# A hybrid decoder trunk: the output projection's low parts pinned behind the conv taps, and the conv finish traced inside the attention

## The chip, the cores and the metric

The kernel runs on one core of a Trainium2 chip. The core has a matrix engine (TensorE, PE in the profile, whose weight loads are listed as PEld), a vector engine (VectorE, DVE), a scalar engine (ScalarE, ACT), a general engine (GpSimd, POOL) and a queue that issues DMAs (SyncE, SP). Every engine works through its own instructions in the order fixed when the program is built; semaphores make one wait for another. The metric is the time of one execution in device microseconds, as the median of several runs.

## The reference

Two layers act on a sequence of 512 rows of 1024 features. Each layer is a half-weighted SwiGLU, a token mixer and a second half-weighted SwiGLU, all residual and behind an RMS norm. The mixer is:

```python
a, g, q, k, v = jnp.split(h @ w_in[l], splits, axis=-1)
conv_out = conv_module(a, g, conv_w[l], conv_b[l], conv_norm[l])
...
diff_out = diff_attention(q, k, v, rel_bias, lam, lam_init, subln_norm[l])
x = x + jnp.concatenate([conv_out, diff_out], axis=-1) @ w_out[l]
```

`conv_module` gates `a` with the sigmoid of `g`, convolves each of 512 channels with its own 31 taps, causally, norms over the channels and applies `silu`. `diff_attention` has four heads; each has two softmax maps over the same 512 positions, causal and with a shared bias, and its value weights are the first map minus `lam` times the second. The result is normed per head. The output projection takes 512 conv features and 512 attention features.

## The kernel before

All matrix products are done in three passes. A weight chunk of 128 x 1024 is loaded (`wraw`), ScalarE writes its rounded high part (`whi`, L97) and VectorE or GpSimd the rest (`wlo`, L98); activations have the same two parts (`acth`, `actl`). `mm3` adds high x high (L160), high x low part of the activations (L163) and low part of the weights x high (L164). Rings hold five raw chunks and four high and four low parts. `chunk` (L100) issues the load on SP's queue and makes both parts.

The mixer first forms the conv inputs and the queries, keys and values. Then `conv_taps` (L652) runs over the four channel tiles: tile 0 wholly on GpSimd (31 taps), tile 3 with 10 taps there, the rest on VectorE. A tap on GpSimd is a product on ScalarE (`prod`, L662, a ring of two) and an add on GpSimd (L663). `conv_square` adds up the squares in `csum` (L650).

The attention is a software pipeline of 16 steps (four blocks of 128 queries from the last to the first, four heads each). `attend(n)` does, for step n, the two score products on PE (`ps_sc`, L709, in the PSUM banks `sc` and `po`), the bias add with a running minimum on VectorE (L713), the exponentials on ScalarE (L717), and the joining of both maps on VectorE (`r2` L720, `c2` L722, then L723); for step n-2 the transposes (`ps_at`, L730, copied by L732), for step n-3 the products with the values (`ps_o`, L739), and after the last head of a block its norm and its transposes into the activations (L766, L768, L769).

`conv_finish` (L684) sums the rows of `csum` by transposes (`rows_rstd`: L216, L220, L221 and a power on GpSimd, L209), spreads the result over the partitions (`spread`: a diagonal on VectorE L236, a product on PE L240, a copy on ScalarE L244), and for each tile scales on GpSimd (L689), takes a tanh on ScalarE (L691), and makes the gated value and its two parts (L692 on VectorE, L693 on ScalarE, L694 on VectorE).

The output projection (L810 on) adds the conv half first, for all rows, in eight tiles (`ps_out`, in the same banks `sc` and `po`, added to `x` by L820), and then the attention half in two row halves. Its weight chunks' low parts are made on GpSimd. After it the next SwiGLU's activations are prepared tile by tile (L257, L258).

The order of the instructions on each engine isn't the order of the text. A planner simulates the program and gives each engine the ready instruction that was traced first, so an instruction that is traced late can be placed early if its inputs are ready and its engine is free in the plan. `keep_in_program_order` pins an instruction behind the one traced just before it on its engine.

Of the kernel before, what the change touches and what calls it, by code (L numbers as in the profile page):

```python
# [15 lines left out]
ALU = mybir.AluOpType  # L16
# [11 lines left out]
CC = 512  # L28
# [39 lines left out]
def trunk(ctx: ExitStack, tc: tile.TileContext, xt, par, lamv, relb, onehot,  # L68
          gu1, dn1, wag, wqkv, wout, gu2, dn2, out):
    nc = tc.nc  # L70
    V, S, G, T = nc.vector, nc.scalar, nc.gpsimd, nc.tensor
# [9 lines left out]
    def f32(ap):  # L81
        return ap.bitcast(F32)
# [3 lines left out]
    def bank(tag, name):  # L86
        return psum.tile([P, 512], F32, tag=tag, name=name, bufs=BANKS[tag])
# [5 lines left out]
        dt = F32 if "raw" in tag else F32R  # L93
        return wp.tile([P, n], dt, tag=tag, name=tag, bufs=RING[tag])

    def parts_of(raw, hi, lo, eng=None):
        S.activation(hi, raw, AF.Copy)  # L97
        (eng or V).tensor_tensor(out=lo, in0=raw, in1=f32(hi), op=ALU.subtract)  # L98

    def chunk(src, eng=None):  # L100
        raw, hi, lo = ring("wraw"), ring("whi"), ring("wlo")
        nc.sync.dma_start(raw, src)
        parts_of(raw, hi, lo, eng)
        return hi, lo

    def gather(src, blocks, eng=None):
# [79 lines left out]
    for k0, k1 in ((0, 1), (1, 4), (4, KT)):  # L186
        h = slice(k0 * P, k1 * P)
# [24 lines left out]
    def rows_rstd(s, dim, use="", pin=False):  # L212

        ps = bank("y", "ps_rows")
        for j in range(NT):
            mm = T.transpose(ps[:, j * P : (j + 1) * P], s[:, j * P : (j + 1) * P], ident)  # L216
            if pin:
                tc.keep_in_program_order(mm)
        v = small.tile([P, NT], F32, tag=f"rowv{use}", name="rowv")
        V.tensor_reduce(v, ps.rearrange("p (j c) -> p j c", j=NT), axis=AX.X, op=ALU.add)  # L220
        V.tensor_scalar(v, v, 1.0 / dim, EPS, op0=ALU.mult, op1=ALU.add)  # L221
        return rsqrt(v, NT, use), v

    def spread(rc, tag, pin=False, split=False):

        parts, dt, left = [rc], F32, ones
        if split:
            hi = small.tile([P, NT], F32R, tag="rc_hi", name="rc_hi")
            V.tensor_scalar(hi, rc, 1.0, None, op0=ALU.mult)
            lo = small.tile([P, NT], F32, tag="rc_lo", name="rc_lo")  # L230
            V.tensor_tensor(lo, rc, f32(hi), op=ALU.subtract)
            parts, dt, left = [f32(hi), lo], F32R, ones_r
        ps = bank("y", "ps_spread")
        for n, part in enumerate(parts):
            dg = tmp.tile([P, NT, P], dt, tag=("diag", "sq")[n], name="diag", bufs=1 + n)
            V.tensor_tensor(  # L236
                dg, ident.unsqueeze(1).broadcast_to([P, NT, P]),
                part.unsqueeze(2).broadcast_to([P, NT, P]), op=ALU.mult,
            )
            mm = T.matmul(ps, left, dg.rearrange("p j c -> p (j c)"), start=n == 0, stop=n == len(parts) - 1)  # L240
            if pin:
                tc.keep_in_program_order(mm)
        r = act.tile([P, SEQ], F32, tag=tag, name=tag)
        S.activation(r, ps, AF.Copy)  # L244
        return r
# [254 lines left out]
    nlam, gq, gsub, ghalf = [], [], [], []  # L500
# [35 lines left out]
    def mixer(l, pr, after):  # L536
        with tc.tile_pool(name="mix", bufs=1) as mp, tc.tile_pool(name="mt", bufs=2) as mt:
# [104 lines left out]
            csum = mp.tile([P, SEQ], F32, tag="csum", name="csum")  # L642
# [9 lines left out]
            def conv_taps(c, n):  # L652

                wc = _AT["conv_w"] + c * TAPS
                yp = None
                if n:
                    yp = mp.tile([P, SEQ], F32, tag="yp%d" % (n < TAPS), name="yp")
                    G.tensor_scalar(yp, us[c][:, 0:SEQ], pars[l][:, wc : wc + 1], col(l, "conv_b", c),
                                    op0=ALU.mult, op1=ALU.add)
                    for t in range(1, n):  # L660
                        p = mt.tile([P, SEQ], F32, tag="prod", name="prod")
                        S.activation(p, us[c][:, t : t + SEQ], AF.Copy, scale=pars[l][:, wc + t : wc + t + 1])  # L662
                        G.tensor_tensor(yp, yp, p, op=ALU.add)  # L663
                if n == TAPS:
                    ys[c] = yp
                    conv_square(c, yp)
                    return
                y = bank("y", "ps_y")
                if not n:
                    V.tensor_scalar(y, us[c][:, 0:SEQ], pars[l][:, wc : wc + 1], col(l, "conv_b", c),  # L670
                                    op0=ALU.mult, op1=ALU.add)
                else:
                    V.tensor_scalar(y, us[c][:, n : n + SEQ], pars[l][:, wc + n : wc + n + 1], None, op0=ALU.mult)
                for t in range(n + 1 if n else 1, TAPS):
                    V.scalar_tensor_tensor(y, us[c][:, t : t + SEQ], pars[l][:, wc + t : wc + t + 1], y,
                                           op0=ALU.mult, op1=ALU.add)
                ys[c] = us[c][:, PAD:]
                if n:
                    V.tensor_tensor(ys[c], y, yp, op=ALU.add)
                else:  # L680
                    S.activation(ys[c], y, AF.Copy)
                conv_square(c, ys[c])

            def conv_finish():  # L684
                rcv = spread(rows_rstd(csum, CC, "c")[0], "rb")
                for c in range(CT):
                    z = ys[c]
                    hg = ghalf[l][:, c : c + 1]
                    G.tensor_tensor(z, z, rcv, op=ALU.mult)  # L689
                    th = mt.tile([P, SEQ], F32, tag="gl", name="th", bufs=1)  # L690
                    S.activation(th, z, AF.Tanh, scale=hg)  # L691
                    V.scalar_tensor_tensor(z, th, 1.0, z, op0=ALU.add, op1=ALU.mult)  # L692
                    S.activation(ch[:, c, :], z, AF.Copy, scale=hg)  # L693
                    V.scalar_tensor_tensor(cl[:, c, :], z, hg, f32(ch[:, c, :]), op0=ALU.mult, op1=ALU.subtract)  # L694
# [5 lines left out]
            def softmaxes(i, h):  # L700
                W = (i + 1) * P
                tq = slice(i * P, W)
                if h == 0:
                    sums[i] = small.tile([P, 2, HEADS], F32, tag="sums", name="sums")
                scs = [bank(tag, "ps_sc")[:, :W] for tag in ("sc", "po")]
                e0 = mt.tile([P, SEQ], F32, tag="e0", name="e", bufs=4)[:, :W]
                sm = sums[i]
                for m in range(2):
                    T.matmul(scs[m], qz[:, m, h, tq], kt[:, h, :W], start=True, stop=True)  # L709

                for m, (sc, e) in enumerate(zip(scs, (e0, scs[1]))):
                    mn = small.tile([P, 1], F32, tag=f"mn{m}", name="mn")
                    V.tensor_tensor_reduce(  # L713
                        out=e, in0=sc, in1=row["bias"][:, h, SEQ - W :], scale=1.0, scalar=3e38,
                        op0=ALU.add, op1=ALU.min, accum_out=mn,
                    )
                    S.activation(e, e, AF.Exp, bias=mn, scale=-1.0, accum_out=sm[:, m, h : h + 1])  # L717

                r2 = small.tile([P, 1], F32, tag="r2", name="r2")
                V.reciprocal(r2, sm[:, 1, h : h + 1])  # L720
                c2 = small.tile([P, 1], F32, tag="c2", name="c2")
                V.tensor_scalar(c2, r2, nlam[l], sm[:, 0, h : h + 1], op0=ALU.mult, op1=ALU.mult)  # L722
                V.scalar_tensor_tensor(e0, scs[1], c2, e0, op0=ALU.mult, op1=ALU.add)  # L723
                maps[i, h] = e0

# [75 lines left out]
                project_values(NT - 2 - 2 * n)  # L801
            for c in range(CT):
                conv_taps(c, POOL_TAPS[c])
            for n in range(2, len(steps) + 5):
                attend(n)
            conv_finish()

            for half, t in ((0, slice(0, SEQ)), (1, slice(SEQ // 2, SEQ)), (1, slice(0, SEQ // 2))):  # L810
                if t.stop == SEQ:
                    w = [None] * 4
                for m in range(KT):
                    if w[m // 2] is None:
                        w[m // 2] = chunk(wout[l, half, m // 2], G)
                    ps = bank(("sc", "po")[m % 2], "ps_out")[:, : t.stop - t.start]
                    for kk in range(4):
                        k = half * 4 + kk
                        mm3(ps, wpart(w[m // 2], (m % 2) * 4 + kk), (ch[:, k, t], cl[:, k, t]), kk == 0, kk == 3)
                    V.tensor_tensor(x[:, m, t], ps, x[:, m, t], op=ALU.add)  # L820

                    if half == 1 and t.start == 0 and m < KT // 2:
                        after(m)
# [103 lines left out]
```

## Time and profile before

| | |
|---|---|
| median of 3 runs | 1797.14 us (1795.66 to 1797.37) |
| the profiled execution | 1795.63 us |
| its span | 1793.9 us, 28355 instructions |
| PE busy | 1783.0 us, 99% |
| DVE, ACT, POOL busy | 67%, 50%, 37% |
| granted TensorE clock | 1.00 |

Times in the rows are microseconds from the start of the span, unless they are given as ns. A timeline row reads: start, length, engine, line, operation, out<-in, form and count, and in brackets the engine's idle time before it and what ended that. A group's row gives the count, then the busy time in us and the mean of one in ns, then the idle time before them. A row of one line's instructions gives the count and the least, median and greatest duration in ns. A row of stretches gives for each engine the busy time in it and the number of instructions.

### The profile page before, as it was taken

The numbers are of one execution on the slowest core, as the hardware profiler recorded it, in microseconds if no ns is written. First come the engines' busy times: TensorE is split into PE (matmuls) and PEld (weight loads), VectorE is DVE, ScalarE is ACT, GpSimd is POOL, SyncE is SP. The second block draws the span as 40 slices with busy tenths as digits, with TensorE's granted clock in tenths as the row PEclk, the third lists the DMA queues.
The fourth block names the chain that finished last, engine by engine and source line by source line (L and its number), as shares of the span: only waits on it lengthen the run. The fifth ranks groups of instructions, "written<-read, shape, count | busy, mean of one in ns | idle before, by whom it ended". The sixth has DMA issues, their size and how long they took to land.

```text
span 1793.9 us, 28355 instructions
## 1 busy us (share of the span) xinstructions
PE 1783.0 (99%) x10845; PEld 1590.0 (89%) x10845; DVE 1207.6 (67%) x1862; ACT 897.1 (50%) x1482; POOL 666.8 (37%) x460
## 2 busy tenths in 40 slices
PE   9999999999999999999999999999999999999999
PEld 7899899888788899899888998998887888998997
DVE  6977476568867867477576764765788587663762
ACT  5555265445844456266433643644558354552651
POOL 4243242269843133133102312412797332422420
PEclk9999999999999999999999999999999999999999
DMA  7466476423212367366334664663231133664651
GB/s 243 109 171 188 108 185 173 123 89 94 71 48 83 94 165 189 105 171 191 104 94 98 171 167 123 178 175 118 71 116 50 48 106 93 166 177 112 180 150 59
DMA packets 111721, 231.24 MB, mean 129 GB/s; under 512 B 12151, under 2 KB 33414, under 8 KB 111584
## 3 DMA queue, kind: packets, MB, share of 16 engines
q1 hardware_dynamic: 91488, 191.93, 33.4%
q0 software_dynamic: 19808, 37.33, 12.8%
q8 instruction: 85, 1.39, 0.3%
q14 instruction: 52, 0.43, 0.1%
q10 hardware_dynamic: 288, 0.16, 0.0%
HBM read 227.26 MB, written 3.42 MB: 129 GB/s over the span
## 4 chain that ended last, share of the span: by engine, by line
PE 96%; DVE 2%; ACT 1%; issue 1%; DMA 0%; ACTq 0%; DVEq 0%
PE ps_pair L379 38%; PE ps_d L164 9%; PE ps_d L160 9%; PE ps_d L163 9%; PE ps_pair L163 5%; PE ps_pair L164 5%; PE ps_pair L160 5%; PE ps_pair L592 2%; PE ps_pair L593 2%; PE ps_pair L591 2%; PE ps_out L160 1%; PE ps_out L163 1%; PE ps_sc L709 1%; PE ps_out L164 1%; DVE actl L258 1%; PE ps_v L623 1%
## 5 line engine op out<-in xcount | busy, mean ns | idle before, releaser
L97 ACT ACTIVATE whi<-wraw 128x512 fp32r<-128x512 f32 (+2 forms) x600 | 467.2, 802 | 607.5 <-PE ps_pair L379 223.2
L98 DVE TENSOR_TENSOR wlo<-wraw,whi 128x512 fp32r<-128x512 f32 (+2 forms) x556 | 521.3, 960 | 212.5 <-ACT whi L97 207.3
L379 PE MATMUL ps_pair<-acth,wlo 128*128 128x256 f32 x1088 | 307.9, 283 | 0.0
L379 PE MATMUL ps_pair<-actl,whi 128*128 128x256 f32 x1088 | 307.9, 283 | 0.0
L379 PE MATMUL ps_pair<-acth,whi 128*128 128x256 f32 x1088 | 307.9, 283 | 0.0
L163 PE MATMUL ps_d<-hl,whi 128*128 128x512 f32 x704 | 273.9, 389 | 0.0
L164 PE MATMUL ps_d<-hh,wlo 128*128 128x512 f32 x704 | 273.0, 389 | 0.0
L160 PE MATMUL ps_d<-hh,whi 128*128 128x512 f32 x704 | 268.4, 389 | 0.0
L143 POOL TENSOR_TENSOR wraw<-wraw 128x512 f32<-128x512 f32 x68 | 112.8, 1658 | 344.6 <-DMA wraw<-in_gu 286.2
L379 PE MATMUL ps_pair<-th,wlo 128*128 128x256 f32 x816 | 230.9, 283 | 0.0
L379 PE MATMUL ps_pair<-tl,whi 128*128 128x256 f32 x816 | 230.8, 283 | 0.0
L379 PE MATMUL ps_pair<-th,whi 128*128 128x256 f32 x816 | 230.8, 283 | 0.0
L138 POOL DMA_DIRECT2D wraw<-in_gu x68 | 82.0, 1205 | 374.9 <-DMA wraw<-in_gu 258.5
L379 PEld LDWEIGHTS ps_pair<-acth,whi 128*128 128x128 f32 x1088 | 208.9, 192 | 0.3
L379 PEld LDWEIGHTS ps_pair<-actl,whi 128*128 128x128 f32 x1088 | 208.9, 192 | 0.3
L379 PEld LDWEIGHTS ps_pair<-acth,wlo 128*128 128x128 f32 x1088 | 208.9, 192 | 0.0
L475 DVE SCALAR_TENSOR_TENSOR x<-ps_d,x 128x512 f32<-128x512 f32 x96 | 64.7, 688 | 180.5 <-PE ps_d L164 180.1
L160 PE MATMUL ps_pair<-acth,whi 128*128 128x512 f32 x448 | 173.8, 392 | 1.4 <-ACT whi L97 1.4
L163 PE MATMUL ps_pair<-actl,whi 128*128 128x512 f32 x448 | 174.7, 391 | 0.3 <-DVE actl L258 0.2
L164 PE MATMUL ps_pair<-acth,wlo 128*128 128x512 f32 x448 | 173.9, 390 | 0.0
L379 PEld LDWEIGHTS ps_pair<-tl,whi 128*128 128x128 f32 x816 | 156.5, 192 | 0.7
L379 PEld LDWEIGHTS ps_pair<-th,whi 128*128 128x128 f32 x816 | 156.5, 192 | 0.6
(174 smaller groups left out, 3268.8 us busy)
## 6 DMA issues: line engine op xcount, KB each, us to landing
wraw<-in_gu SPq DMA_DIRECT2D x208, 256.0 KB, 4.1
wraw<-in_gu SPq DMA_DIRECT2D x104, 512.0 KB, 3.7
wraw<-in_gu POOLq DMA_DIRECT2D x68, 512.0 KB, 5.8
wraw<-in_wqkv SPq DMA_DIRECT2D x24, 512.0 KB, 3.6
wraw<-in_dn SPq DMA_DIRECT2D x84, 128.0 KB, 3.1
wraw<-in_dn SPq DMA_DIRECT2D x32, 256.0 KB, 3.0
wraw<-in_wag SPq DMA_DIRECT2D x16, 512.0 KB, 3.6
wraw<-in_wout SPq DMA_DIRECT2D x16, 512.0 KB, 3.7
```

The lines of the kernel that those rows point to most:

```text
L97: S.activation(hi, raw, AF.Copy)
L98: (eng or V).tensor_tensor(out=lo, in0=raw, in1=f32(hi), op=ALU.subtract)
L138: nc.gpsimd.dma_start(two.rearrange("p (b c) -> p b c", b=2), u[:, h[0]].unsqueeze(1).broadcast_to([P, 2, 512]), accum_op=ALU.add)
L143: G.tensor_tensor(more[:, h[0]], two[:, h[1]], whole[:, h[0]], op=ALU.add)
L160: first = T.matmul(ps, wh, xh, start=start, stop=False)
L163: T.matmul(ps, wh, xl, start=False, stop=False)
L164: T.matmul(ps, wl, xh, start=False, stop=stop)
L379: mm = T.matmul(ps, l, r, start=first and i == j == 0, stop=False, skip_group_check=True)
L475: V.scalar_tensor_tensor(x[:, m, :], ps, 0.5, x[:, m, :], op0=ALU.mult, op1=ALU.add)
L591: T.matmul(ps[n], xh[:, t], wh, start=k == 0, stop=False)
L592: T.matmul(ps[n], xh[:, t], wl, start=False, stop=False)
L593: T.matmul(ps[n], xl[:, t], wh, start=False, stop=k == KT - 1)
```

## The change

Three things change. First, `parts_of` and `chunk` can pin the low part's instruction. The four chunks of the output projection's conv half are made ahead of it: two right after the row sums of the conv group, two at step 9 of the attention, all with their low parts pinned on GpSimd. Second, the row sums of the conv group (`conv_rows`) are traced right after the taps, and the rest of `conv_finish` after `attend(9)`, where both stood behind the last step. Third, the factor of the second map, `c2`, is made with `scalar_tensor_tensor` on two tensors and one per-partition scalar, where it was `tensor_scalar` with two per-partition scalars.

```diff
-    def parts_of(raw, hi, lo, eng=None):
+    def parts_of(raw, hi, lo, eng=None, pin=False):
         S.activation(hi, raw, AF.Copy)
-        (eng or V).tensor_tensor(out=lo, in0=raw, in1=f32(hi), op=ALU.subtract)
-
-    def chunk(src, eng=None):
+        low = (eng or V).tensor_tensor(out=lo, in0=raw, in1=f32(hi), op=ALU.subtract)
+        if pin:
+            tc.keep_in_program_order(low)
+
+    def chunk(src, eng=None, pin=False):
         raw, hi, lo = ring("wraw"), ring("whi"), ring("wlo")
         nc.sync.dma_start(raw, src)
-        parts_of(raw, hi, lo, eng)
+        parts_of(raw, hi, lo, eng, pin)
         return hi, lo
...
-            def conv_finish():
-                rcv = spread(rows_rstd(csum, CC, "c")[0], "rb")
+            def conv_rows():
+                return rows_rstd(csum, CC, "c")[0]
+
+            def conv_finish(rcv):
+                rcv = spread(rcv, "rb")
...
-                V.tensor_scalar(c2, r2, nlam[l], sm[:, 0, h : h + 1], op0=ALU.mult, op1=ALU.mult)
+                V.scalar_tensor_tensor(c2, r2, nlam[l], sm[:, 0, h : h + 1], op0=ALU.mult, op1=ALU.mult)
...
             for c in range(CT):
                 conv_taps(c, POOL_TAPS[c])
+
+            rcv = conv_rows()
+            wo = [chunk(wout[l, 0, n], G, pin=True) for n in range(2)]
             for n in range(2, len(steps) + 5):
                 attend(n)
-            conv_finish()
+                if n == 9:
+                    conv_finish(rcv)
+                    wo += [chunk(wout[l, 0, n], G, pin=True) for n in range(2, 4)]
...
             for half, t in ((0, slice(0, SEQ)), (1, slice(SEQ // 2, SEQ)), (1, slice(0, SEQ // 2))):
                 if t.stop == SEQ:
-                    w = [None] * 4
+                    w = [None] * 4 if half else wo
```

## The prediction

> **What bounds the kernel now.** I read the page first, then the busy time by stretches around the attention, then TensorE's (PE's) groups and starts in the stretch that stood out, then GpSimd's (POOL's) order of work ahead of it.
>
> ```profile
> span 1793.9 us, 28355 instructions
> ...
> PE 1783.0 (99%) x10845; PEld 1590.0 (89%) x10845; DVE 1207.6 (67%) x1862; ACT 897.1 (50%) x1482; POOL 666.8 (37%) x460
> ```
>
> PE is busy for 1783.0 of 1793.9 us. The change takes no matmul away, so all it can win is time in which PE stands or is fed too slowly. Three stretches of layer 0's attention, and the middle one again in layer 1:
>
> ```profile
> core 0: us, PE busy (x) PEld busy (x) DVE busy (x) ACT busy (x) POOL busy (x), PEclk, DMA share, GB/s
> 472.05:490.00 17.95, 17.52 (x97) 12.66 (x96) 13.90 (x49) 15.88 (x42) 15.36 (x11) 1.00 0.40 119
> 490.00:501.05 11.05, 9.53 (x64) 7.61 (x62) 10.85 (x42) 8.40 (x28) 5.72 (x5) 1.00 0.00 0
> 501.05:512.00 10.95, 10.66 (x57) 8.23 (x58) 10.95 (x34) 8.84 (x26) 2.94 (x5) 1.00 0.01 1
> 1380.84:1391.89 11.05, 9.53 (x64) 7.60 (x62) 10.84 (x42) 8.40 (x28) 5.72 (x5) 1.00 0.01 1
> ```
>
> The recorded idle time of PE is 0.43, 1.52 and 0.29 us in layer 0; layer 1 repeats the middle stretch (1.52 again), so I work out one layer and double it. VectorE (DVE) is full in the middle stretch (10.85 of 11.05) and in the one after it, where PE nevertheless loses little. The ends of matmuls are modelled, so I also count the work itself: PE's groups between 472.04 and 501.07 us, and a few starts from its timeline.
>
> ```profile
> L739 PE MATMUL ps_o<-vv,at 128*128 128x128 f32 x64 | 9.0, 278 | 0.2 <-ACT at L732 0.2
> L709 PE MATMUL ps_sc<-kt,qz 128*128 128x384 f32 x16 | 6.2, 487 | 0.0
> L730 PE MATMUL ps_at<-ident,e 128*128 128x128 f32 x34 | 5.6, 276 | 0.5 <-ACT at L732 0.4
> L709 PE MATMUL ps_sc<-kt,qz 128*128 128x256 f32 x16 | 4.6, 382 | 0.0
> L709 PE MATMUL ps_sc<-kt,qz 128*128 128x512 f32 x8 | 3.8, 592 | 0.0
> L709 PE MATMUL ps_sc<-kt,qz 128*128 128x128 f32 x10 | 1.9, 285 | 0.0
> L240 PE MATMUL ps_spread<-diag,ones 128*128 128x512 f32 x2 | 1.0, 594 | 0.0
> L216 PE MATMUL ps_rows<-ident,csum 128*128 128x128 f32 x4 | 0.6, 272 | 0.0
> L766 PE MATMUL ps_o<-ident,ov 128*128 128x128 f32 x4 | 0.6, 272 | 0.0
> ```
>
> ```profile
> 472.05 1.88 PE L709 MATMUL ps_sc<-kt,qz 128*128 128x512 f32 x4
> 473.76 0.60 PE L730 MATMUL ps_at<-ident,e 128*128 128x128 f32 x4
> 474.20 2.53 PE L709 MATMUL ps_sc<-kt,qz 128*128 128x512 f32 x6
> ...
> 501.08 0.49 PE L160 MATMUL ps_out<-acth,whi 128*128 128x512 f32 x1 [1.26 <-ACT acth L693]
> ```
>
> From start to start, four 512-wide scores take 1.71 us (0.43 each), four 128-wide transposes 0.44 (0.11 each). The 116 matmuls of 128 columns then hold 12.8 us, the 10 of 512 hold 4.3, and in proportion the 16 of 384 hold 5.1 and the 16 of 256 hold 3.4: 25.6 us of work in the 29.0 us from 472.05 to 501.08. So 3.4 us per layer are lost ahead of the first matmul of the output projection. That matmul is the first filler that does not hang on a softmax, and it waits for the conv group's finish (L693). Why the finish is late stands on POOL:
>
> ```profile
> 469.30 2.42 POOL L98 TENSOR_TENSOR wlo<-wraw,whi 128x1024 fp32r<-128x1024 f32 x1
> ...
> 472.91 4.71 POOL L98 TENSOR_TENSOR wlo<-wraw,whi 128x1024 fp32r<-128x1024 f32 x2
> ...
> 478.82 2.35 POOL L98 TENSOR_TENSOR wlo<-wraw,whi 128x1024 fp32r<-128x1024 f32 x1
> ...
> 483.92 1.27 POOL L663 TENSOR_TENSOR yp<-yp,prod 128x512 f32<-128x512 f32 x1 [0.16 <-ACT prod L662]
> 487.40 1.27 POOL L650 TENSOR_TENSOR csum<-csum,csq 128x512 f32<-128x512 f32 x1 [2.21 <-ACT csq L649]
> ...
> 491.51 1.01 POOL L209 TENSOR_TENSOR rs_y<-rowv,mhalf 128x4 f32<-128x4 f32 x1 [1.58 <-DVE rowv L221]
> 496.35 1.28 POOL L689 TENSOR_TENSOR yp<-yp,rb 128x512 f32<-128x512 f32 x1 [3.82 <-ACT rb L244]
> 497.58 3.64 POOL L689 TENSOR_TENSOR u<-u,rb 128x512 f32<-128x512 f32 x3
> ```
>
> Four low parts of the output weights, 2.42 + 4.71 + 2.35 = 9.5 us, run among the last conv adds, long before any ps_out. Behind the last add come the sum of squares (ends 488.67), the power, the spread, and the four scalings L689.
>
> **Part 1, the pinned low parts.** They go behind the power of the conv rows (L209). The work is the same, and no add, activation or DMA is new. The conv sum can come earlier by 9.5 us at most, by nothing if ScalarE's products (prod, L662) hold the adds anyway. The last add waited 0.16 us for its product, so I take a place near the upper end: 7.5 us. Given back: the first two low parts (4.7 us) now stand between the power and the scalings, where POOL had 3.82 us idle, so the scalings wait 0.9 us, and perhaps half of a softmax block's own power on POOL (an L209 like the one of 1.01 us): about 1.5 us. The first ps_out moves from 501.1 to about 495. The other two low parts run behind the four scalings (4 x 1.25 us, then 4.7 us, so about 502 at the latest); they are wanted only by the third pair of output tiles, behind the 48 matmuls of the first two pairs. The raw weights' ring of five is held longer, so on SP's queue the loads of the second half's chunks and, behind them, of the next stage's first weights are issued later. ScalarE reads the first such chunk at 514.42, and that one has the fifth place of the ring; I cost the move at nothing. If that cover were gone it would cost one landing, 3.7 us:
>
> ```profile
> 514.42 1.06 ACT L97 ACTIVATE whi<-wraw 128x1024 fp32r<-128x1024 f32 x1 [2.22 <-PE ps_out L163]
> ```
>
> ```profile
> wraw<-in_wout SPq DMA_DIRECT2D x16, 512.0 KB, 3.7
> ```
>
> **Part 2, the finish traced at step 9 of the attention.** It gives the finish the way ahead of softmax steps 10 to 15 on ScalarE, DVE and PE. It adds no instruction; the steps behind it come later by what it takes. That is covered by the filler: in 501.05 to 512.00, finish and softmax already run together with DVE full, and PE loses 0.29 us.
>
> **Part 3, one instruction for the scale.** L722 is one instruction before, too:
>
> ```profile
> L722 DVE TENSOR_SCALAR c<-r,nlam,sums x32: 260/269/275, 463.8 to 1402.3; 128x1 f32<-128x1 f32 x32
> ```
>
> ```profile
> L746 DVE SCALAR_TENSOR_TENSOR se<-sums x8: 135/157/191, 477.5 to 1396.2; 128x4 f32<-128x4 f32 x8
> ```
>
> The new form is that of L746 with a per-partition scalar. Bounds: 157 ns, or no gain (269). I take 0.21, so 0.06 x 16 = 1 us of DVE per layer, of which half falls where DVE is full: 0.4 us.
>
> **The sum, per layer.** Of the 11 us from 490.0, 6 become filled. Their loss: of the 3.4 us, 0.43 lie ahead of 490 and 1.26 are the stand at the first ps_out, and the other 1.7 spread over 11 us, so 0.9 for 6 us. Half of the 1.26 stays, since PE's order is fixed when the program is built and the head of the finish may be late again: 0.6 won. Part 3 gives 0.4, and of the losses behind the first ps_out some 0.4 go, as the four parts of the finish follow closer. 0.9 + 0.6 + 0.4 + 0.4 = 2.3, so 4.6 us for two layers. The profiled execution took 1795.63 us (span 1793.9 and 1.7 around it), which gives 1791.0. It stands 1.5 below the median of the runs, 1797.14; against the median the sum is 1792.5, which I predict. 0.2% of the time, 3.6 us, is about what a measurement of this kernel can tell from no change.
>
> **The rivals.**
>
> *POOL's work moves beside DVE's and holds it (slower).* A DVE operation on two tensors in SBUF is longer beside a busy POOL:
>
> ```profile
> L692 DVE SCALAR_TENSOR_TENSOR u<-th,u x6: 669/679/681, 501.9 to 1398.8; 128x512 f32<-128x512 f32 x6
> L692 DVE SCALAR_TENSOR_TENSOR yp<-th,yp x2: 1301/1301/1301, 499.0 to 1389.8; 128x512 f32<-128x512 f32 x2
> ```
>
> The two of 1301 ns start at 499.0, among the L689 of POOL; the six of 679 run later. So 0.62 us is the wait for one POOL operation of 1.25. Where the low parts ran before, DVE read scores from PSUM; now they and the scalings stand beside the finish. The spread's diagonal (L236, two SBUF tensors), ready just as the first low part starts, would wait up to 2.3 us, and three more L692 0.62 each: 4.1 us on the finish's chain. The new L722 reads two SBUF tensors too and can wait in each of 16 steps. If PE's order counts on the earlier finish, PE stands for the 4.1 us: less the 1.7 won elsewhere (0.9 + 0.4 + 0.4), +2.4 per layer, 1802 us. It decides once the lateness is over the 2.3 won. Against it: POOL is done with this work within about 17 us, and a late finish also leaves softmax work to run. [...]
>
> *The conv sum is not earlier, or PE was fed anyway (no change).* Scalar products may pace the adds, since their ring holds two and ScalarE is 88% busy (15.88 of 17.95). Then the first ps_out stays within 1.5 us of 501; what part 3 wins goes for the 0.9 us of the scalings. 1797, give or take 2.
>
> *All of the loss goes.* If PE is fed from 472 on, the 3.4 and the 0.29 us go, and all of part 3's 1.0: 4.7 per layer, 1787.7.
>
> **How the numbers follow.** The forecast has 0.42 (1789 to 1795 as its own range), the full gain 0.08, no change 0.20, the held DVE 0.25, and 0.05 is left for an order on PE that turns out worse than that, since every queue's order in this block is planned anew. Faster than 1793.5: 0.50, same 0.20, slower 0.30. For 8 in 10 the range goes from 1786 to 1803.5: the full gain and the held DVE, each with the 1.5 us by which the profiled execution and the median differ.
>
> **What would show it.** Right: the four L98 on POOL stand behind the L209 of the rows, the last csum add ends near 481 (488.7 before), the first ps_out in layer 0 starts near 495, PE's idle time between 472 and 512 falls from 2.24 us to about 1, L722 falls to about 0.21 us. Wrong: csum still ends near 488; or L236, L692 or the new L722 take 1 us or more with POOL busy beside them, and a ps_out or transpose on PE waits for ACT at L693 or L732 for longer than 1.3 us. Work between the two mixers should be unchanged.

## The result, and the profile after

The changed kernel takes 1809.55 us (median of 4 runs, 1808.40 to 1810.07) and the kernel before, beside it, 1796.40 (1795.56 to 1797.37). The ratio is 1.0072, with a 95% interval from 1.0059 to 1.0084: 13 us slower, where 4.6 us faster was forecast, and outside the range. The profiled execution took 1808.4 us, with a span of 1806.6.

The page of the profile after, its totals:

```profile
span 1806.6 us, 28351 instructions
...
PE 1788.7 (99%) x10845; PEld 1594.4 (88%) x10845; DVE 1217.1 (67%) x1862; ACT 897.8 (50%) x1482; POOL 669.0 (37%) x460
```

The totals hardly show it. The stretches of layer 0's attention do (columns as in the prediction; PE's busy time and PEclk are the ones to look at):

```profile
core 0: us, PE busy (x) PEld busy (x) DVE busy (x) ACT busy (x) POOL busy (x), PEclk, DMA share, GB/s
472.00:490.00 18.00, 17.66 (x96) 12.48 (x94) 15.12 (x42) 15.32 (x38) 10.61 (x8) 1.00 0.04 5
490.00:501.00 11.00, 8.48 (x48) 6.11 (x48) 10.82 (x34) 7.74 (x22) 8.20 (x8) 1.00 0.24 89
501.00:512.00 11.00, 7.93 (x36) 6.62 (x37) 10.33 (x29) 6.68 (x23) 5.56 (x4) 0.69 0.34 97
512.00:530.00 18.00, 18.00 (x91) 15.01 (x90) 9.11 (x26) 6.71 (x16) 4.05 (x4) 1.00 0.00 0
```

PE stands 0.34 + 2.52 + 3.07 = 5.93 us between 472 and 512, where it stood 2.24 before: 3.7 us more. Besides, its granted clock is 0.69 on the mean from 501 to 512, where it was 1.00 before. The two together account for the loss, as an estimate: 0.31 of the clock over the 7.93 busy us is 2.5 us, and 3.7 + 2.5 = 6.2 us per layer, against 12.7 us for two layers between the two spans.

What POOL does, in its timeline of the kernel after:

```profile
480.56 1.27 POOL L652 TENSOR_TENSOR csum<-csum,csq 128x512 f32<-128x512 f32 x1 [2.74 <-ACT csq L651]
485.28 1.02 POOL L211 TENSOR_TENSOR rs_y<-rowv,mhalf 128x4 f32<-128x4 f32 x1 [3.44 <-DVE rowv L223]
486.26 4.67 POOL L98 TENSOR_TENSOR wlo<-wraw,whi 128x1024 fp32r<-128x1024 f32 x2
...
494.93 1.27 POOL L694 TENSOR_TENSOR yp<-yp,rb 128x512 f32<-128x512 f32 x1 [1.17 <-ACT rb L246]
496.16 3.71 POOL L694 TENSOR_TENSOR u<-u,rb 128x512 f32<-128x512 f32 x3
499.84 5.11 POOL L98 TENSOR_TENSOR wlo<-wraw,whi 128x1024 fp32r<-128x1024 f32 x2
```

The order is the intended one. The conv sum ends at 481.83, 6.8 us earlier than before. Now DVE, whose lines carry new numbers (`se` was L746, the diagonal L236, the gated value L692, `c2` L722; the first matmuls of the projection were L160):

```profile
486.43 2.21 DVE L751 SCALAR_TENSOR_TENSOR se<-sums 128x4 f32<-128x4 f32 x1
488.90 2.57 DVE L238 TENSOR_TENSOR diag<-ident,rs_y 128x512 f32<-128x512 f32 x1
...
496.68 0.59 DVE L727 SCALAR_TENSOR_TENSOR c<-r,nlam,sums 128x1 f32<-128x1 f32 x1
...
502.67 2.83 DVE L697 SCALAR_TENSOR_TENSOR u<-th,u 128x512 f32<-128x512 f32 x1
...
505.50 0.27 DVE L718 CUSTOM_DVE_ANT_0 e<-ps_sc,bias 128x128 f32<-128x128 f32 x1
```

The diagonal in the kernel before, for comparison (the rows of `se`, of the gated value and of `c2` before stand in the prediction):

```profile
492.64 0.69 DVE L236 TENSOR_TENSOR diag<-ident,rs_y 128x512 f32<-128x512 f32 x1
```

The reader should lay this over POOL's rows. `se` is an operation on 512 numbers and took 0.157 us before; here it begins 0.2 us after the first low part has begun and ends at 488.64, where that low part ends (486.26 and half of 4.67). The diagonal begins behind it and waits for the second low part (to 490.9). The gated value begins half a microsecond after the fourth low part has begun (502.2) and ends at 505.50, half a microsecond after that one's end (504.95). On DVE the bias add of the next scores, L718, stands behind it, and PE behind that. PE's timeline:

```profile
503.03 0.97 PE L744 MATMUL ps_o<-vv,at 128*128 128x128 f32 x4 [1.11 <-ACT at L737]
505.82 1.52 PE L714 MATMUL ps_sc<-kt,qz 128*128 128x128 f32 x4 [1.82 <-DVE mn L718]
...
510.28 0.48 PE L162 MATMUL ps_out<-acth,whi 128*128 128x512 f32 x1
```

PE's longest waits, over both layers (total, count, longest). First the one that led before, the stand of the projection for the conv finish, then those of the kernel after:

```profile
PE ps_out L160 <- ACT acth L693: 2.5, 2, 1.3
```

```profile
PE ps_sc L714 <- DVE mn L718: 4.8, 4, 2.1
PE ps_spread L242 <- DVE diag L238: 3.6, 2, 1.8
PE ps_o L744 <- ACT at L737: 2.2, 2, 1.1
```

The projection starts at 510.28, 9.2 us later than before. It is not the finish that holds it (its first tile was ready at 500.10, before at 501.03) but the softmax work ahead of it in PE's order, which DVE feeds late.

### The profile page after: what moved, and what is told of

It reads as the page before. It is cut to its first block, busy times and chain, and to the rows that moved or that the text cites. A ratio compares the mean times of both kernels' runs of the same rounds, so it can differ in the third digit from the quotient of the medians.

```text
span 1806.6 us, 28351 instructions
## 1 busy us (share of the span) xinstructions
PE 1788.7 (99%) x10845; PEld 1594.4 (88%) x10845; DVE 1217.1 (67%) x1862; ACT 897.8 (50%) x1482; POOL 669.0 (37%) x460
## 4 chain that ended last, share of the span: by engine, by line
PE 95%; DVE 4%; issue 0%; ACT 0%; DMA 0%; ACTq 0%; DVEq 0%
PE ps_pair L381 38%; PE ps_d L165 9%; PE ps_d L162 9%; PE ps_d L166 9%; PE ps_pair L165 5%; PE ps_pair L166 5%; PE ps_pair L162 5%; PE ps_pair L595 2%; PE ps_pair L593 2%; PE ps_pair L594 2%; PE ps_out L162 1%; PE ps_out L165 1%; PE ps_out L166 1%; PE ps_sc L714 1%; DVE actl L260 1%; PE ps_v L625 1%
## 5 line engine op out<-in xcount | busy, mean ns | idle before, releaser
L97 ACT ACTIVATE whi<-wraw 128x512 fp32r<-128x512 f32 (+2 forms) x600 | 466.5, 802 | 604.2 <-PE ps_pair L381 227.8
L145 POOL TENSOR_TENSOR wraw<-wraw 128x512 f32<-128x512 f32 x68 | 105.7, 1554 | 348.9 <-DMA wraw<-in_gu 286.5
```

The costliest lines, as they stand in the source:

```text
L145: G.tensor_tensor(more[:, h[0]], two[:, h[1]], whole[:, h[0]], op=ALU.add)
```

## The experiments

Five theories. **A**: the pinned low parts read SBUF on POOL while DVE has operations on two tensors in SBUF, and DVE waits. **B**: the finish traced at step 9 spoils the order on PE. **C**: the new form of the scale, which reads two tensors, is what waits. **D**, formed after the first results: even without holds the projection can't start early, since its tiles take turns in the PSUM banks `sc` and `po` with the scores, which are traced earlier. **E**, the rival of D: the order on PE or the load of DVE sets that start, and not the banks.

The profiled executions differ by up to 2 us in what lies ahead of the attention (its first score starts between 457.3 and 459.4), so the table counts from the first score product of layer 0: to the first `ps_out`, and to the last first-pass `ps_out` of that layer (the block). "Stands" is PE's idle time from 455 to 575 us, "clock" the granted clock there.

| kernel | first ps_out | block | stands | clock | median us | ratio to before (95%) |
|---|---|---|---|---|---|---|
| before | 43.6 | 94.4 | 2.40 | 1.00 | 1796.40 | 1 |
| after | 52.6 | 100.5 | 6.08 | 0.97 | 1809.55 | 1.0072 (1.0059 to 1.0084) |
| e1, scale alone | 45.2 | 95.4 | 2.64 | 1.00 | 1797.17 | 1.0006 (0.9997 to 1.0015) |
| e2, after, old scale | 52.0 | 100.1 | 5.87 | 0.97 | 1806.91 | 1.0057 (1.0045 to 1.0070) |
| e3, finish alone | 43.6 | 94.4 | 2.37 | 1.00 | 1795.92 | 0.9999 (0.9991 to 1.0008) |
| e4, pins alone | 52.0 | 100.3 | 5.09 | 0.96 | 1807.33 | 1.0059 (1.0045 to 1.0072) |
| e5, after, unpinned | 45.2 | 95.4 | 2.65 | 1.00 | 1796.80 | 1.0005 (0.9996 to 1.0014) |
| e6, after, POOL does not read | 44.2 | 93.5 | 2.20 | 1.00 | 1794.35 | 0.9992 (0.9983 to 1.0001) |
| e7, after, DVE one SBUF input | 45.2 | 94.4 | 2.83 | 1.00 | 1796.35 | 1.0002 (0.9993 to 1.0010) |
| e8, before, DVE one SBUF input | 44.2 | 93.9 | 2.36 | 1.00 | 1794.74 | 0.9995 (0.9986 to 1.0004) |
| e9, after, own bank | 39.8 | 95.9 | 2.96 | 0.99 | 1800.23 | 1.0025 (1.0017 to 1.0034) |
| e10, before, own bank | 43.6 | 93.0 | 1.98 | 1.00 | 1792.42 | 0.9982 (0.9973 to 0.9990) |
| e11, e6 with own bank | 39.2 | 91.5 | 0.99 | 1.00 | 1791.41 | 0.9975 (0.9966 to 0.9985) |
| e12, first pair pinned | 44.0 | 97.9 | 3.54 | 0.97 | 1803.30 | 1.0041 (1.0027 to 1.0055) |
| e13, after, in quarters | 47.8 | 101.6 | 7.79 | 0.97 | 1812.08 | 1.0090 (1.0076 to 1.0104) |
| e14, e13 with own bank | 38.7 | 96.6 | 4.93 | 1.00 | 1803.02 | 1.0039 (1.0027 to 1.0052) |
| e15, before, own bank for six | 43.6 | 96.4 | 3.98 | 1.00 | 1799.91 | 1.0021 (1.0012 to 1.0030) |

**One part at a time.** Each of the first three kernels has one part of the change or lacks one.

The scale alone, in the kernel before:

```diff
-                V.tensor_scalar(c2, r2, nlam[l], sm[:, 0, h : h + 1], op0=ALU.mult, op1=ALU.mult)
+                V.scalar_tensor_tensor(c2, r2, nlam[l], sm[:, 0, h : h + 1], op0=ALU.mult, op1=ALU.mult)
```

> The kernel before with part 3 alone: c2 by scalar_tensor_tensor. Theory A (a VectorE operation with two SBUF tensors is held by the GpSimd operation beside it, and what holds most are the pinned low parts of 2.4 us): the low parts run among the conv adds as before, so c2 is held by an add's rest at most, some 0.4 us in four or five of the 16 steps per layer, against 0.05 us saved in the others: within 3 us of the kernel before. Theory B (the finish ahead of the softmax steps starves TensorE, whatever GpSimd does): within 1 us of before. Theory C (the new form of c2 itself is what costs): about 13 us slower, like the whole change.

Measured 1.0006, no difference that can be told from none; C's 13 us are not there. The changed kernel with the old scale (the same diff the other way):

> The changed kernel without part 3: c2 by tensor_scalar again. Theory A: the long waits of the changed kernel's VectorE (2.21 us in L751, 2.57 in L238, 2.83 in L697) stay, only the short ones of c2 (0.67, 0.59, 0.42) go: 1 to 3 us faster than the changed kernel, so 9 to 12 us slower than before. Theory B: the same 13 us slower as the changed kernel. Theory C: as fast as before.

Measured 1806.91 against 1809.55: beside the pins the new form costs some 2.6 us (the two intervals overlap), and over ten of the thirteen are left without it. C explains about a fifth, and only where A is at work.

The finish alone, shown against the changed kernel (the old scale is back too):

```diff
-            wo = [chunk(wout[l, 0, n], G, pin=True) for n in range(2)]
+            wo = [None] * 4
             for n in range(2, len(steps) + 5):
                 attend(n)
                 if n == 9:
                     conv_finish(rcv)
-                    wo += [chunk(wout[l, 0, n], G, pin=True) for n in range(2, 4)]
```

> Part 2 alone: row sums and conv finish are traced where the changed kernel has them; the output projection's weight chunks are made where they were, unpinned, and c2 is as before. Theory A: no low part runs beside the finish, so no wait over 1.3 us on VectorE; TensorE is not starved and its clock stays whole: 3 us faster to 3 us slower than before. Theory B: at least 8 us slower, with TensorE's clock halved for some us in each layer.

Measured 0.9999, with the first `ps_out` and the block exactly as before. Tracing the finish earlier changes nothing by itself, and B falls. The next kernel, which has the pins without it, confirms this. The pins alone, again against the changed kernel with the old scale:

```diff
                 if n == 9:
-                    conv_finish(rcv)
                     wo += [chunk(wout[l, 0, n], G, pin=True) for n in range(2, 4)]
+            conv_finish(rcv)
```

> Part 1 alone: row sums early, the four low parts pinned (two behind the row sums' power, two at step 9), the finish after the last step as before, and c2 as before. Theory A: the first two low parts still stand where the small product se (L751 of the changed kernel) and the spread's diagonal come up, so waits of some 2 us on VectorE are seen, but the other two are less likely to meet a finish: 3 to 10 us slower. Theory B: no slower than before, rather 2 to 5 us faster, since the conv sum is some 7 us earlier.

Measured 1807.33, 11.5 us over the 1795.83 of the kernel before beside it: as slow as e2, which has the early finish too, so part 1 is nearly the whole loss. It is more than the 3 to 10 us that A allowed: the second pair met the finish after all. Its timeline of POOL, then that of DVE:

```profile
487.59 5.14 POOL L98 TENSOR_TENSOR wlo<-wraw,whi 128x1024 fp32r<-128x1024 f32 x2
...
498.93 5.11 POOL L98 TENSOR_TENSOR wlo<-wraw,whi 128x1024 fp32r<-128x1024 f32 x2
```

```profile
487.48 0.15 DVE L751 SCALAR_TENSOR_TENSOR se<-sums 128x4 f32<-128x4 f32 x1
488.02 2.49 DVE L238 TENSOR_TENSOR diag<-ident,rs_y 128x512 f32<-128x512 f32 x1
...
499.53 2.29 DVE L697 SCALAR_TENSOR_TENSOR u<-th,u 128x512 f32<-128x512 f32 x1
```

Here `se` falls just ahead of the low parts and takes 0.15 us; the diagonal and the gated value fall beside them and take 2.49 and 2.29. Which operation is hit differs between the two kernels; that some are hit doesn't.

The pins taken off, all else of the change kept:

```diff
-            wo = [chunk(wout[l, 0, n], G, pin=True) for n in range(2)]
+            wo = [chunk(wout[l, 0, n], G) for n in range(2)]
...
-                    wo += [chunk(wout[l, 0, n], G, pin=True) for n in range(2, 4)]
+                    wo += [chunk(wout[l, 0, n], G) for n in range(2, 4)]
```

> The changed kernel with the four chunks traced where it has them, but not pinned: the planner may put the low parts among the conv adds again. Theory A: it does, no low part stands beside the finish, and the long waits on VectorE go: within 4 us of the kernel before. Theory B: as slow as the changed kernel, 10 us or more.

Measured 1.0005: the low parts go back among the conv adds, the conv sum is late again, and the loss is gone.

**Is it the reading?** Two kernels leave POOL's work where the pins put it and take away one side of the conflict each. In the first, each pinned low part is replaced by two fills:

```diff
-        low = (eng or V).tensor_tensor(out=lo, in0=raw, in1=f32(hi), op=ALU.subtract)
         if pin:
-            tc.keep_in_program_order(low)
+            tc.keep_in_program_order(G.memset(f32(lo), 0.0))
+            G.memset(f32(lo), 0.0)
+        else:
+            (eng or V).tensor_tensor(out=lo, in0=raw, in1=f32(hi), op=ALU.subtract)
```

> The changed kernel with each of the four pinned low parts replaced by two fills of the low part's tile on GpSimd, which write it and read nothing from SBUF; the low parts of these four chunks are left out of the result. GpSimd stays busy at the same places, for about 1 to 2 us per low part. Theory A, in the form that only reads collide: L751 and L238 run at their 0.16 and 0.69 us beside the fills, and so does L697; TensorE's clock stays whole: 1790 to 1798 us. If GpSimd's mere occupation, or the order on TensorE, is what costs: 1804 us or more.

Measured 0.9992. Its timelines of POOL, of DVE and of PE:

```profile
486.34 0.96 POOL L99 MEMSET wlo<- 128x1024 f32 x1
487.36 0.95 POOL L100 MEMSET wlo<- 128x1024 f32 x1
...
491.20 1.27 POOL L696 TENSOR_TENSOR yp<-yp,rb 128x512 f32<-128x512 f32 x1
```

```profile
486.53 0.16 DVE L753 SCALAR_TENSOR_TENSOR se<-sums 128x4 f32<-128x4 f32 x1
486.95 0.69 DVE L240 TENSOR_TENSOR diag<-ident,rs_y 128x512 f32<-128x512 f32 x1
```

```profile
501.88 0.47 PE L164 MATMUL ps_out<-acth,whi 128*128 128x512 f32 x1
```

`se` starts 0.1 us later than in the changed kernel, with POOL just as busy beside it, and takes 0.16 us in place of 2.21. POOL's work is a little shorter here (3.8 us for a pair of low parts, not 4.7), so the second kernel keeps the low parts as they are and changes DVE's side: `se` and the diagonal go to ScalarE, and the tanh and the gated value stand in PSUM, so that DVE reads one tensor from SBUF.

```diff
-            V.tensor_tensor(
-                dg, ident.unsqueeze(1).broadcast_to([P, NT, P]),
-                part.unsqueeze(2).broadcast_to([P, NT, P]), op=ALU.mult,
-            )
+            if on_act:
+                for j in range(NT):
+                    S.activation(dg[:, j, :], ident, AF.Copy, scale=part[:, j : j + 1])
+            else:
...
-                    th = mt.tile([P, SEQ], F32, tag="gl", name="th", bufs=1)
+                    th = bank("y", "ps_th")
...
-                    V.scalar_tensor_tensor(z, th, 1.0, z, op0=ALU.add, op1=ALU.mult)
+                    V.scalar_tensor_tensor(th, th, 1.0, z, op0=ALU.add, op1=ALU.mult)
...
-                V.scalar_tensor_tensor(c2, r2, nlam[l], sm[:, 0, h : h + 1], op0=ALU.mult, op1=ALU.mult)
+                V.tensor_scalar(c2, r2, nlam[l], sm[:, 0, h : h + 1], op0=ALU.mult, op1=ALU.mult)
...
-                V.scalar_tensor_tensor(se, sums[i][:, 0, :], VD * EPS, sums[i][:, 0, :], op0=ALU.mult, op1=ALU.mult)
+                S.activation(se, sums[i][:, 0, :], AF.Square, scale=math.sqrt(VD * EPS))
```

> The changed kernel with VectorE's operations on two SBUF tensors taken out of this block: se as a square on ScalarE, the spread's diagonal as four scaled copies on ScalarE, tanh and the gated value in PSUM, and c2 by tensor_scalar. GpSimd keeps all four pinned low parts. Theory A: no wait over 1 us is left on VectorE, the conv sum's 7 us stay won, and the clock stays whole: 1788 to 1796 us. Theory B: still 1804 us or more, since the finish is still ahead of the softmax steps.

Measured 1.0002: POOL's low parts are there, at full length, and cost nothing that can be measured. The gain that the expectation allowed for the early conv sum (down to 1788) isn't there either.

```profile
486.75 4.69 POOL L98 TENSOR_TENSOR wlo<-wraw,whi 128x1024 fp32r<-128x1024 f32 x2
...
497.07 4.65 POOL L98 TENSOR_TENSOR wlo<-wraw,whi 128x1024 fp32r<-128x1024 f32 x2
```

The same replacements in the kernel before, as the control (its diff is that of e7 without `c2`):

> The kernel before with the same replacements of two-tensor operations as the run beside it. Theory A: before has a single such wait of 0.62 us per layer in the finish, so it gains 0 to 2 us and loses up to 2 by the four copies on ScalarE: 1794 to 1799 us. It is the measure for what the replacements alone do.

Measured 0.9995: by themselves they are worth nothing that can be measured. So either side of the conflict, taken away, takes the 13 us away, and A is shown. In the rows, `se` took 2.21 us beside low parts that read SBUF (the kernel after) and 0.16 beside fills that only write it (e6).

**Why the early conv sum wins so little.** In e6 the holds are gone and the sum is early (first tile of activations ready at 496.55), yet the projection starts 44.2 us after the first score, no earlier than the 43.6 of before. Theory D: its tiles use the banks of the scores. So the first four tiles of the conv half were given the bank `y`, which the conv part has left by then. In the kernel before:

```diff
-                    ps = bank(("sc", "po")[m % 2], "ps_out")[:, : t.stop - t.start]
+                    ps = bank("y" if half == 0 and m < 4 else ("sc", "po")[m % 2], "ps_out")[:, : t.stop - t.start]
```

> The kernel before with the same four output tiles in bank y. Theory D: in before the first ps_out waits for the conv finish itself (row of 1.26 us), so the start stays at 501; scores keep their double banks, and it gains 0 to 4 us. Theory E: 1795 to 1798 us.

Measured 1792.42, ratio 0.9982 (0.9973 to 0.9990): this one line, without any of the change, is 3.5 us faster than before, and no other kernel here that does all of the work beats it. The start is where it was, since the conv sum is late, but the block is 1.4 us shorter. Only 0.4 of these are fewer stands of PE (1.98 for 2.40); what the rest is, these runs don't show. The same in e6:

> The changed kernel with the four pinned low parts replaced by fills that read no SBUF (these four low parts are left out of the result), and the first four output tiles in bank y. Theory D: the first ps_out moves from 501.9 to about 497, near the first conv tile's activations at 496.6, and the time falls from 1794.4 to 1787 to 1792 us. Theory E: 1793 to 1797 us.

Measured 1791.41, 4.5 us under before, with the projection at 39.2 us. The matmuls of the projection's first pass in layer 0 (count, shortest, median and longest in ns, first and last start), of this kernel and of the kernel before:

```profile
L164 PE MATMUL ps_out<-acth,whi x96: 274/283/502, 496.8 to 549.2; 128*128 128x256 f32 x64, 128*128 128x512 f32 x32
```

```profile
L160 PE MATMUL ps_out<-acth,whi x96: 277/283/501, 501.1 to 551.9; 128*128 128x256 f32 x64, 128*128 128x512 f32 x32
```

e11 differs from e6 in that one line, and its projection starts 5.1 us earlier: D is shown, and E falls. So the first `ps_out`, at 496.8, is near the 495 of the forecast once both obstacles are out of the way; neither was in its sum. The time is near the forecast too, but not by the forecast's working: the bank alone gave 3.5 us without the early conv sum (e10), and the early sum adds 1.0 to it (1791.41 against 1792.42, with intervals that overlap). D needs A out of the way. With the own bank in the changed kernel (old scale; `se` and the diagonal on ScalarE as in e7, but the tanh in SBUF, since the bank is taken):

> The changed kernel with c2 as before, se and the spread's diagonal on ScalarE, tanh in SBUF, and the first four output tiles of the conv half in the PSUM bank y, which is free after the spread, instead of the scores' banks. Theory D (with the holds gone, the output projection starts late because it shares its two PSUM tags with the scores, which are traced first): the first ps_out starts within 2 us of the first conv tile's activations, near 496 us, TensorE loses less in the attention, and the time is 1786 to 1793 us. Theory E (the order on TensorE or VectorE's load sets the start, not the banks): the first ps_out stays at 500 or later and the time at 1795 to 1800 us.

```profile
494.28 1.52 DVE L701 SCALAR_TENSOR_TENSOR yp<-th,yp 128x512 f32<-128x512 f32 x1
...
497.83 1.79 DVE L703 SCALAR_TENSOR_TENSOR actl<-yp,ghalf,acth 128x512 fp32r<-128x512 f32 x1
...
499.89 2.51 DVE L701 SCALAR_TENSOR_TENSOR u<-th,u 128x512 f32<-128x512 f32 x1
```

Measured 1800.23. The projection starts at 39.8 us, as D has it, but not the time. The first gated value (494.28) falls among the scalings; the activations' low part behind it (497.83) and the second gated value (499.89) fall beside the second pair of low parts, which runs from 496.72 to 501.85. The block is 95.9 us: the start is won and lost again behind it. Last, six tiles in the bank `y` in place of four, in the kernel before (`m < 6`):

> The kernel before with six output tiles of the conv half in bank y instead of four. Theory D: the scores keep both banks for longer, but one bank for all makes each tile wait for the last one's add (0.7 us): 1790 to 1794 us. If one bank too long starves TensorE at the end: 1794 to 1798 us.

```profile
530.38 0.50 PE L160 MATMUL ps_out<-acth,whi 128*128 128x512 f32 x1 [0.67 <-DVE x L820]
539.93 0.39 PE L160 MATMUL ps_out<-acth,whi 128*128 128x256 f32 x1 [0.92 <-ACT whi L97]
```

Measured 1799.91, slower than four tiles by 7.5 us and outside both ranges. `y` is a single bank, and a tile in it waits for the add of the tile ahead to `x`: 0.67 us in the first row. PE stands 2.0 us longer than with four tiles; the wait for a high part of the weights (0.92, second row), which four tiles don't have, is a larger share of it. The block is 3.4 us longer, and what makes up the rest is open.

**Can the early low parts be kept?** Two kernels keep them in another form. First, only the first two low parts pinned:

```diff
-                    wo += [chunk(wout[l, 0, n], G, pin=True) for n in range(2, 4)]
+                    wo += [None] * 2
```

(with the old scale)

> The changed kernel with c2 as before and with only the first two low parts made early and pinned; the other two are made where they were before, unpinned. Theory A: the wait of the spread's diagonal (2.5 us) stays, that of L697 (2.3 us) goes unless another low part falls beside it; the clock stays whole or nearly so: 2 to 7 us slower than before, against 10 to 11 for all four. Theory B was already without support.

```profile
485.83 9.78 POOL L98 TENSOR_TENSOR wlo<-wraw,whi 128x1024 fp32r<-128x1024 f32 x4
```

Measured 1803.30, 7.4 us over the kernel before beside it, and the clock is not whole (0.97). All four stood in one row now, since the unpinned pair moved up behind the pinned one, and the scalings waited for them until 495.70 (496.35 before: the early sum was lost as well). Second, each pinned low part cut in four, so that DVE would wait for a quarter at most:

```diff
-        low = (eng or V).tensor_tensor(out=lo, in0=raw, in1=f32(hi), op=ALU.subtract)
-        if pin:
-            tc.keep_in_program_order(low)
+        for c in range(4 if pin else 1):
+            c = slice(c * 256, (c + 1) * 256) if pin else slice(0, raw.shape[-1])
+            low = (eng or V).tensor_tensor(out=lo[:, c], in0=raw[:, c], in1=f32(hi[:, c]), op=ALU.subtract)
+            if pin:
+                tc.keep_in_program_order(low)
```

> The changed kernel with each pinned low part cut into four operations of 256 columns, at the same place and with the same work (some 0.6 us each). Theory A, by the length of one operation: a held VectorE operation waits out 0.6 us and not 2.3, so L751, L238 and L697 stay under 1.5 us, TensorE's clock stays whole or nearly so, and the time is 1795 to 1800 us. If reading as such were what holds VectorE (it gets in only when GpSimd is done with all its work), the waits stay at 2 us and over and the time at 1805 to 1811 us.

Its timelines of POOL and of DVE:

```profile
487.96 5.99 POOL L100 TENSOR_TENSOR wlo<-wraw,whi 128x256 fp32r<-128x256 f32 x8
...
498.43 6.87 POOL L100 TENSOR_TENSOR wlo<-wraw,whi 128x256 fp32r<-128x256 f32 x8
```

```profile
488.98 0.95 DVE L240 TENSOR_TENSOR diag<-ident,rs_y 128x512 f32<-128x512 f32 x1
...
497.89 1.14 DVE L699 SCALAR_TENSOR_TENSOR yp<-th,yp 128x512 f32<-128x512 f32 x1
...
501.05 1.17 DVE L701 SCALAR_TENSOR_TENSOR actl<-yp,ghalf,acth 128x512 fp32r<-128x512 f32 x1
502.14 1.21 DVE L699 SCALAR_TENSOR_TENSOR u<-th,u 128x512 f32<-128x512 f32 x1
```

Measured 1812.08, which missed the expectation. No single operation of DVE in these rows takes over 1.21 us any more, but a quarter takes 0.75 us on the mean in the first pair and 0.86 in the second, where a fourth of a whole low part would be 0.6. A pair of low parts now takes 6.0 and 6.9 us where it took 4.7 and 5.1, and more of DVE's operations fall beside it, one behind the other. PE waits longer for the bias add than in the changed kernel (7.9 us over both layers, where that had 4.8):

```profile
PE ps_sc L716 <- DVE mn L720: 7.9, 4, 2.5
```

The length of one POOL instruction alone is not the price. With the own bank beside it (and the old scale):

> The same cut, with c2 as before and the first four output tiles in PSUM bank y. With theories A and D: the first ps_out near 497 us and 1789 to 1794 us, at or below the kernel before with the bank alone (1792.4). Otherwise 1796 us or more.

Measured 1803.02, well over the 1789 to 1794 of A and D. The projection starts early (38.7), the clock stays whole, and PE still stands 2.5 us longer than before in the layer (4.93 against 2.40), beside a block that is 2.2 us longer.

## Why the prediction was wrong

The step that failed is a term that the sum put at nothing: DVE held by the pinned low parts. It stands only among the rivals, at a chance of 0.25 and a price of 4.8 us. Measured, the pins alone cost 11.5 us (e4), and the loss is gone when these low parts don't read SBUF (e6) or DVE's operations beside them have one SBUF input (e7). A second step failed behind it, and alone it would have kept most of the gain away: the first `ps_out` follows its input. Step by step:

- *What bounds the kernel.* Right: the stretch between 490 and 512 decides, DVE is full there, and the change acts there.
- *Part 1, the conv sum.* Right: 7.5 us earlier was said, 6.8 measured.
- *Part 1, the delay of the scalings.* Here the first failed step acts: about 1.5 us were taken off, for low parts in the scalings' way on POOL. POOL was free: it stood 1.17 us ahead of the first scaling, which waited for the spread. From the end of the power to the end of the diagonal it took 5.2 us (486.30 to 491.47), where it took 0.8 before (492.52 to 493.33), since `se`, ahead of the diagonal on DVE, and the diagonal were each held. So the scalings began at 494.93, just 1.4 us earlier than before (496.35): 5.4 of the 6.8 us were gone at this place. In e6, without holds, the sum is 6.7 us earlier and the scalings begin at 491.20, 5.2 earlier: 1.6 are gone, as forecast.
- *Part 1, the first `ps_out` near 495.* The second step that failed. The sum let it follow its input. In e6 the input was early and the projection wasn't: its banks were shared with the scores (e9, e11 and e14 start it at 38.7 to 39.8 us, all other kernels at 43.6 or later). So even with nothing held the 2.3 us per layer did not come: e6 is 1.5 us faster for two layers, and its interval reaches no change.
- *Part 1, DMAs.* Right: in both kernels PE waits for a high part (L97) just once, at the very start (0.7 us after, 1.4 before), and never in or behind the attention.
- *Part 2 at nothing.* Right: e3 is 0.9999. That DVE was full and PE lost little there was read as cover for more work on DVE; that held for the finish, not for holds of 2 us each.
- *Part 3.* The size was right: 0.21 us predicted, a median of 0.219 measured. The gain, 0.4 us per layer, is too small for e1 to tell, and beside the pins the new form costs some 2.6 us, as it can be held (0.59 in the row above).
- *The rival of the held DVE.* The right mechanism, at a chance of 0.25 and at 1802. What was mis-sized: it counted four waits on the finish's chain, 2.3 for the diagonal and 0.62 for each of three gated values. The diagonal was 1.9 us over its 0.69, as said; `se` was another 2.05 over, and one gated value 2.15 over, behind the second pair of low parts and not behind a scaling of 1.25. The rival put these on the conv finish. They fell on the softmax as well, which shares DVE, and that is what PE waited for (L714 for the bias add, 4.8 us over both layers). The clock was in neither the sum nor the rival: 2.5 us of the 6.2 per layer by the estimate above.

How the 13 us divide between PE's stands and its clock is argued from the windows and only partly shown. e14 has holds with a whole clock and a block longer by 2.2 us; no kernel here has a slow clock without holds. Why quarters are worse than whole low parts, beyond POOL's longer time and the longer wait for the bias add, stays open too.

## What to carry to other kernels

When work is moved on GpSimd, list the VectorE operations with two SBUF inputs that now run beside it, down to the smallest, and price each, as an estimate, at the rest of the GpSimd instruction: here `se`, of 0.157 us, took 2.21, and the diagonal, of 0.69, took 2.57, beside low parts of 2.35 (cutting that instruction up did not lower the price here: 1812.08 us, against 1809.55). Then ask who stands behind them on VectorE. Where VectorE is full, don't count an earlier input as an earlier result: here it was busy for 10.82 of 11.00 us, the conv sum came 6.8 us earlier, and the projection 9.2 us later. And before an input is made earlier, look whether its consumer has a PSUM bank of its own: here that one line gave 3.5 us, and the moved work gave nothing that could be measured without it.

## What was not expected of the hardware

**The clock fell without one long stand.** Stretches of the kernel after around the fall (columns as above):

```profile
500.00:503.30 3.30, 1.72 (x11) 1.26 (x11) 3.30 (x10) 2.66 (x10) 3.30 (x2) 1.00 0.06 7
503.34:510.16 6.82, 4.89 (x21) 4.08 (x20) 6.45 (x21) 3.18 (x8) 3.22 (x3) 0.50 0.51 153
```

The granted clock is 1.00 to 503.3 and 0.50 for the 6.8 us behind it. In the 3.3 us ahead of the fall PE's longest stand is the 1.11 us of the row at 503.03, and PE is busy for 1.72 us; none of its waits anywhere near is over 2.1 us. Low recorded activity is not all of it either, since e14 kept its clock through a thinner stretch:

```profile
500.00:503.00 3.00, 1.23 (x7) 0.81 (x6) 3.00 (x10) 2.73 (x10) 3.00 (x4) 1.00 0.00 0
```

In the clock records of the traces of before and after, the changes lie whole multiples of 3.413 us apart, to 0.01 us. In the kernel after the clock is whole from 4.99 us, halves at 503.33 (146 of these steps on), is whole again at 510.16 (2 on), halves in layer 1 at 1401.04 (261 on) and is whole again at 1407.86 (2 on). In the kernel before it is whole from 3.95 to 1792.54 (524 steps), 1.4 us ahead of the span's end. In other kernels the half-speed time of layer 0, estimated from the mean clock of the stretches from 490 to 530, is 3.5 us in e9, 6.8 in e2, e12 and e13, and some 10 in e4.

How much work PE had ahead of a fall is an estimate, by the distance from start to start as in the prediction (0.11 us for 128 columns; for 512 of the projection 0.23, as from 510.60 to 510.83 in the kernel after). In the last step ahead of the two falls of the kernel after, from 499.92 and from 1397.63, ten and eleven matmuls of 128 columns start: 0.32 and 0.35 of 3.41 us. In the kernel before, the thinnest steps of its two mixers, from 498.88 and from 1389.76, hold ten of 128 columns and one of 512 each, 0.39, and the clock stayed whole. What makes the clock fall is not shown: no run here was made to test it.

**A tiny operation took as long as the rest of a low part.** `se`, 128 x 4, went from 0.157 to 2.21 us; `c2`, 128 x 1, from 0.22 to 0.59. It goes the other way too: in the kernel after, the last scaling on POOL begins at 498.26, just behind a gated value on DVE (498.24, 0.68 us, not held), and takes 1.62 us where the first took 1.27.
